# A two-layer trunk kernel: the first 1024 hidden features of each MLP computed plainly, and the recursion's activation operands made during the product that follows

## The chip, the cores and the metric

The kernel runs on one core of a Trainium2 chip. The core has a matrix engine (TensorE, rows PE for matmuls and PEld for weight loads), three elementwise engines (VectorE as DVE, ScalarE as ACT, GpSimd as POOL), and a queue engine (SyncE as SP) from which this kernel issues nearly all its DMAs. Each engine works through its own instructions in order; semaphores tie the engines together. The metric is the device time of one execution in microseconds (us): the median of several runs. A separate, profiled execution gives the trace.

## The reference

A token matrix of 640 tokens (128 context, 512 latent) and 1024 channels passes two layers: a gating mixer in layer 0, an RWKV-7 mixer in layer 1, and after each mixer an MLP with 4096 hidden features. Only the MLP matters here:

```
h = _rmsnorm(x, P['norm2_g'][l]) * (1 + sc2) + sh2
x = x + g2 * (jnp.square(jax.nn.relu(h @ P['mlp_w1'][l])) @ P['mlp_w2'][l])
```

`mlp_w1` is 1024 x 4096, `mlp_w2` 4096 x 1024. Everything is float32.

## The kernel before

**Precision.** Each float32 operand is split into a high part (a cast on ACT into a narrower matmul type) and a low part (a subtraction on DVE). A product is then three matmuls: high x high, high x low, low x high. `mm` issues these three; `split_w` splits weights, `put` splits activations.

**Blocks.** `mlp` walks over the 4096 hidden features in four blocks of 1024. For each block it makes the hidden features (the first product, with `w1`), squares them after a ReLU into `ss`, and multiplies by the block's part of `w2` (the second product, tiles `second_mm`, results added to the residual by `second_out`, L284). A tile is 128 features. A plain tile costs 8 chunks of 128 channels x 3 matmuls x 2 token halves (256 and 384 tokens, `HS`) = 48 matmuls.

**The recursion.** Most of the first product is done by one step of a fast 2x2 matrix recursion: two tiles (a `Pair` of 256 features) come from 7 instead of 8 half-size products, in `pair`, each 4 chunks x 3 matmuls of 320 tokens, together 84 matmuls of 320 columns in place of 96 of 320 columns on average. It needs sums and differences of weight quarters (made on POOL, L475 to L478, and split on ACT and DVE, L452 and L453) and of activation quarters. The activation quarters are made once per layer, in `combos`: for each of four chunk pairs j an add of high and low parts on POOL (m = 0) and on DVE (m = 1), both L596, four DVE adds or subtractions of 320 columns (L600), and a split of 1280 columns back into the tile `Th[j]` (L562 on ACT, L563 on DVE).

**Block 0 before.** Four tiles are plain: in layer 0 tiles 0 to 2 together and then tile 3, in layer 1 tiles 0 and 1 together (`n0`, the number of weight tiles that the previous stage has split already) and then 2 and 3. Then `combos` is called (after the first `n0` tiles in the program), tile 3's results are squared by `first_out` (L626, L627, L562, L563), and features 512 to 1023 come from two pairs, q = 2 and 3. Blocks 1 to 3 use four pairs each. Normalized activations enter in two halves, by `enter`; channel chunks 0 to 3 stand in tiles of their own (`upper`, names ahi and alo), chunks 4 to 7 in slots 1 and 2 of `Th` (name th).

**What sets the order.** Weight tiles go through 5 raw buffers (names wraw), a ring of 3 split buffers (`ring`; names shi and slo, in layer 1 also w1s), and `need(k, i, more)` splits weights ahead by `more` steps. PSUM has three banks `fmps`. The tile framework orders each engine's instructions by priority and readiness in its own model, so the order on an engine is not the order of the source. The scratch `SC` (name bs) holds the normalized activations in `enter` and then the sums of `combos` (half of it for even j, half for odd j).

Of the kernel before, what the change touches and what calls it, by code (L numbers as in the profile page):

```python
# [7 lines left out]
F32 = mybir.dt.float32  # L8
# [7 lines left out]
P = 128  # L16
T = 640
TP = 128
HS = ((0, 256), (256, 640))
KT = 8  # L20
# [8 lines left out]
def tile_trunk(ctx: ExitStack, tc: tile.TileContext, a: dict):  # L29
    nc = tc.nc  # L30
    vec = nc.vector
    act = nc.scalar
# [62 lines left out]
    def parts(pool, tags=("ah", "al")):  # L95
        return pool.tile([P, T], F32R, tag=tags[0], name="ahi"), pool.tile([P, T], F32R, tag=tags[1], name="alo")
# [327 lines left out]
    def mlp(norm, l, ring=None, pre=()):  # L424

        cut = ((0, N2), (N2, T)) if l == 0 else ((N2, T), (0, N2))

        B11, B12, B21, B22 = (0, 1, 2, 3) if l == 0 else (1, 0, 3, 2)
        o0, o1 = (0, 1) if l == 0 else (1, 0)

        SLOT = {1: 0, 2: 1 + l, 3: 2 - l, 5: 3 + B12, 6: 3 + B11, 7: 3 + B22, 4: 3 + B21}
        with ExitStack() as es:
            raw = Pool(es, f"mr{l}", {"r": RAW})
            sp = Pool(es, f"mlps{l}", {"ah": 8, "al": 8})
# [7 lines left out]
            tp = Pool(es, f"mq{l}", {"s": 2})  # L442
            Th = [Pool(es, f"mh{l}{j}", {"t": 1}).tile([P, 2, 7, N2], F32R, "t", "th") for j in range(4)]
# [74 lines left out]

            n0 = len(pre) or 3
            units = []  # L520
            for n in range(4):
                units.append(("p", 0, n, Tile(a["w1"][l, n] if n >= len(pre) else None)))
            units += [("q", 0, q, Pair(0, q)) for q in (2, 3)]
            for b in range(4):
                if b:
                    units += [("q", b, q, Pair(b, q)) for q in range(4)]
# [20 lines left out]
            def need(k, i, more):  # L547
                p = where[k, i] + more
                while count["made"] < len(todo) and count["made"] <= p:
                    ahead()  # L550
                    u, i1, k1, before = todo[count["made"]]
                    for d in before:
                        count["free"] += d.make(0)[1]
                        ahead()
                    made[k1, i1], f = u.make(i1)
                    count["free"] += f
                    count["made"] += 1
                ahead()
# [5 lines left out]

            at = lambda j, i: (Th[j][:, 0, i], Th[j][:, 1, i])

            upper = [parts(sp) for _ in range(4)]
            SC = scr.tile([P, 8, N2], F32, "s", "bs")
            flat = SC.rearrange("p s t -> p (s t)")

            def row(k, t0, t1):
                if k < 4:
                    return [x[:, t0:t1] for x in upper[k]]
                return [Th[k - 4][:, z, 1:3].rearrange("p s t -> p (s t)")[:, t0:t1] for z in range(2)]

            def enter(h):
                r0, r1 = HS[h]
# [7 lines left out]

            def combos():
                for j in range(4):
                    h, w = (y[:, cut[0][0]:cut[0][1]] for y in upper[j])
                    act.copy(Th[j][:, 0, 0], h)
                    vec.tensor_copy(Th[j][:, 1, 0], w)  # L590
                for j in range(4):
                    E = SC[:, 4 * (j % 2):4 * (j % 2) + 4]
                    x = E.rearrange("p s t -> p (s t)")
                    for m in range(2):
                        h, w = row(j + 4 * m, 0, T)
                        (vec if m else nc.gpsimd).tensor_tensor(out=x[:, T * m:T * m + T], in0=h, in1=w, op=ALU.add)  # L596

                    for o, i0, i1, op in ((B22, B22, B12, ALU.subtract), (B12, B12, B11, ALU.subtract),
                                          (B11, B22, B11, ALU.add), (B21, B21, B11, ALU.subtract)):
                        vec.tensor_tensor(out=E[:, o], in0=E[:, i0], in1=E[:, i1], op=op)  # L600
                    put((Th[j][:, 0, 3:7], Th[j][:, 1, 3:7]), E)
# [20 lines left out]
                mm(ps[:, PS0 + t0:PS0 + t1], chunk(w, k), row(k, t0, t1), k == 0, k == 7)  # L622

            def first_out(n, ps, r):
                c = tmps[n % 2][:, 0:r[1] - r[0]]
                act.activation(out=c, in_=ps[:, PS0 + r[0]:PS0 + r[1]], func=AF.Relu)  # L626
                vec.tensor_tensor(out=c, in0=c, in1=c, op=ALU.mult)  # L627
                if n not in ss:
                    ss[n] = parts(sp)
                put([y[:, r[0]:r[1]] for y in ss[n]], c)  # L630
# [46 lines left out]
            need(0, 0, 2)  # L677
            enter(o0)
            fs = [bank() for _ in range(n0)]
            tmps = [tp.tile([P, 512], F32, "s", "ct") for _ in range(2)]  # L680
            ws = [made.pop((m, m)) for m in range(n0)]
            for k in range(KT):
                for m in range(n0):
# [5 lines left out]
            for m in range(n0):  # L689
                first_out(m, fs[m], HS[o0])  # L690
# [3 lines left out]
            for m in range(n0):  # L694
                for k in range(4, KT):
                    first_mm(fs[m], ws[m], k, o1)
                first_out(m, fs[m], HS[o1])
                need(m, m, 3)
            combos()
            for m in range(n0, 4):  # L700
                need(m, m, 1 if m == 3 else 2)
                w, ps = made.pop((m, m)), bank()
                for h in (o0, o1):
                    for k in range(KT):
                        first_mm(ps, w, k, h)
                for h in (o0, o1):
                    first_out(m, ps, HS[h])


            k = 4  # L710
            while k < len(units):
                kind, b, n, u = units[k]
                if kind == "q":
# [5 lines left out]
                if b < 3 or n < 5:  # L719
                    need(k, n, 2)  # L720
                    w, ps = made.pop((k, n)), bank()
# [1198 lines left out]
    with ExitStack() as es:  # L1920
# [15 lines left out]
        for h in (1, 0):  # L1936
            t0, t1 = HS[h]
# [90 lines left out]
```

## Time and profile before

| what | value |
|---|---|
| median of 3 runs (lowest, highest) | 2103.75 us (2103.6, 2108.88) |
| profiled execution, whole | 2122.6 us |
| its span, first to last instruction | 2120.8 us |
| mean granted TensorE clock | 0.927 |
| busy: PE, DVE, ACT, POOL | 92%, 65%, 40%, 27% of the span |
| chain that ended last: PE, DVE, issue, POOL, ACT | 73%, 13%, 5%, 4%, 4% |

The profiled execution took 18.85 us (0.9%) longer than the median of the timed runs. A row of the stage view gives a stretch in us, its length, then for each engine busy time and count, then the granted TensorE clock (1.00 is full), the DMA share and GB/s. A row of the timeline gives start, length, engine, line, operation, what is written from what, and in brackets the idle time before it with what ended it. A row of a group gives busy time and mean ns, a row of a line's view the smallest, median and largest ns. Matmuls overlap, so the pace of TensorE is read from starts and not from lengths. The first MLP stands at 236 to 720 us, the second from 1644 us to the end.

### The profile page before, as it was taken

How to read it: one execution, taken by the hardware profiler on the slowest of the kernel's cores; microseconds unless marked ns; L12 is line 12 of the kernel's file. 1: busy time of each engine (PE TensorE's matmuls, PEld its weight loads, DVE VectorE, ACT ScalarE, POOL GpSimd, SP SyncE). 2: the span in 40 equal slices, each digit the busy share in tenths (PEclk: the TensorE clock that was granted, in tenths of full speed). 3: DMA queues.
4: the chain of work that ended last, by engine and by line, in shares of the span. 5: the costliest groups of instructions: out<-in, count | busy, mean ns of one | idle time of the engine just before them, and what ended most of it. 6: DMA issues, size and time to landing. Idle time of an engine off the chain costs nothing.

```text
span 2120.8 us, 39445 instructions
## 1 busy us (share of the span) xinstructions
PE 1955.6 (92%) x15546; PEld 1696.3 (80%) x15546; DVE 1372.7 (65%) x2706; ACT 853.2 (40%) x1983; POOL 570.6 (27%) x809
## 2 busy tenths in 40 slices
PE   6999969999999879888869999999999799999997
PEld 4777869999999759777657766767787689999997
DVE  5435594646556696765786577787657865656574
ACT  5313542423233255544424445554434633323241
POOL 0000030302030110477642374465301222221210
PEclk9999989999999889987878879998799899999999
DMA  8776103142413124554565445552241122213121
GB/s 282 266 262 223 59 30 100 60 149 70 145 55 129 61 78 137 149 153 145 161 182 155 141 130 167 161 163 77 67 130 60 50 90 69 91 61 99 52 88 50
DMA packets 124442, 254.59 MB, mean 120 GB/s; under 512 B 24417, under 2 KB 63969, under 8 KB 124129
## 3 DMA queue, kind: packets, MB, share of 16 engines
q1 hardware_dynamic: 123824, 251.62, 37.0%
q8 instruction: 122, 2.00, 0.4%
q14 instruction: 64, 0.52, 0.1%
q10 hardware_dynamic: 432, 0.46, 0.1%
HBM read 214.67 MB, written 45.22 MB: 123 GB/s over the span
## 4 chain that ended last, share of the span: by engine, by line
PE 73%; DVE 13%; issue 5%; POOL 4%; ACT 4%; DMA 1%; SPq 0%; POOLq 0%; DVEq 0%; ACTq 0%
PE fmps L114 27%; PE fmps L615 9%; PE zps L311 5%; PE p L1202 4%; PE wops L1472 3%; PE vps L1043 2%; PE za L1331 2%; PE za L1318 2%; PE sy L1345 2%; DVE slo L453 2%; DVE cs L607 1%; PE sy L1326 1%; PE rps L114 1%; PE trps L1224 1%; PE adaps L1458 1%
## 5 line engine op out<-in xcount | busy, mean ns | idle before, releaser
L615 PE MATMUL fmps<-th,shi 128*128 128x320 f32 (+2 forms) x1144 | 258.6, 314 | 28.6 <-ACT ct L626 17.8
L284 DVE SCALAR_TENSOR_TENSOR x<-fmps,mod,x 128x128 f32<-128x128 f32 (+2 forms) x153 | 74.6, 527 | 289.4 <-PE fmps L114 289.4
L615 PEld LDWEIGHTS fmps<-th,shi 128*128 128x128 f32 x1144 | 193.5, 190 | 36.7 <-ACT ct L626 18.1
L452 ACT CAST shi<-wraw 128x1024 fp32r<-128x1024 f32 (+1 forms) x139 | 112.0, 824 | 234.6 <-PE fmps L114 158.8
L615 PE MATMUL fmps<-th,slo 128*128 128x320 f32 (+2 forms) x572 | 178.3, 312 | 0.2 <-DVE slo L453 0.2
L453 DVE TENSOR_TENSOR slo<-wraw,shi 128x1024 fp32r<-128x1024 f32 (+1 forms) x139 | 143.1, 1032 | 30.2 <-ACT shi L452 29.4
L114 PE MATMUL fmps<-ahi,shi 128*128 128x256 f32 (+1 forms) x640 | 151.7, 310 | 0.0
L114 PE MATMUL fmps<-ahi,slo 128*128 128x256 f32 (+1 forms) x640 | 150.9, 309 | 0.0
L114 PE MATMUL fmps<-alo,shi 128*128 128x256 f32 (+1 forms) x640 | 150.9, 309 | 0.0
L114 PE MATMUL fmps<-ahi,w1s 128*128 128x256 f32 (+1 forms) x768 | 148.3, 309 | 0.0
L475 POOL TENSOR_TENSOR s<-wraw 128x512 f32<-128x512 f32 x28 | 38.0, 1360 | 408.4 <-DMA wraw<-w 376.0
L615 PE MATMUL fmps<-th,w1s 128*128 128x320 f32 (+2 forms) x828 | 129.1, 313 | 12.9 <-ACT ct L626 8.9
L615 PEld LDWEIGHTS fmps<-th,w1s 128*128 128x128 f32 x828 | 123.9, 190 | 15.2 <-ACT ct L626 9.2
L1133 POOL TENSOR_TENSOR inv<-inv 128x220 f32<-128x220 f32 (+29 forms) x217 | 100.1, 461 | 114.4 <-DVE inv L1126 57.7
L114 PEld LDWEIGHTS fmps<-ahi,w1s 128*128 128x128 f32 x768 | 127.2, 188 | 0.1
L114 PEld LDWEIGHTS fmps<-ahi,shi 128*128 128x128 f32 x640 | 116.5, 188 | 4.2 <-issue 2.5
L1202 PE MATMUL p<-W,IT 128*128 128x256 f32 x320 | 109.5, 453 | 10.0 <-DVE B L1217 6.0
L114 PEld LDWEIGHTS fmps<-alo,shi 128*128 128x128 f32 x640 | 116.9, 188 | 0.0
L114 PEld LDWEIGHTS fmps<-ahi,slo 128*128 128x128 f32 x640 | 116.9, 188 | 0.0
L1135 POOL TENSOR_TENSOR inv<-inv 128x220 f32<-128x220 f32 (+29 forms) x217 | 106.3, 490 | 16.9
L452 ACT CAST w1s<-wraw 128x512 fp32r<-128x512 f32 (+1 forms) x71 | 57.3, 815 | 132.0 <-PE fmps L114 105.6
L615 PEld LDWEIGHTS fmps<-th,slo 128*128 128x128 f32 x572 | 108.9, 190 | 0.6 <-DVE slo L453 0.6
(345 smaller groups left out, 5042.4 us busy)
## 6 DMA issues: line engine op xcount, KB each, us to landing
wraw<-w SPq DMA_DIRECT2D x126, 512.0 KB, 3.6
wraw<-ada SPq DMA_DIRECT2D x64, 512.0 KB, 4.5
W<-dKR SPq DMA_DIRECT2D x80, 256.0 KB, 3.5
adaw<-adac SPq DMA_DIRECT2D x32, 512.0 KB, 4.4
dKR<-zero SPq DMA_DIRECT2D x32, 320.0 KB, 6.1
dKR<-KR SPq DMA_DIRECT2D x32, 320.0 KB, 4.1
dIT<-IT SPq DMA_DIRECT2D x16, 640.0 KB, 3.4
IT<-dIT SPq DMA_DIRECT2D x80, 128.0 KB, 2.7
```

Of the source, the lines that this page charges most:

```text
L114: pe.matmul(ps[:, PS0 + t0:PS0 + t1], w, x[:, t0:t1], start=start, stop=stop)
L284: vec.scalar_tensor_tensor(out=X[n][:, t0:t1], in0=ps[:, t0 - r[0]:t1 - r[0]], scalar=mod[l][:, which, n, g:g + 1], in1=X[n][:, t0:t1], op ...
L311: pe.matmul(pss[i], x[:, i * P:(i + 1) * P], w[:, kq * 512:(kq + 1) * 512], start=(k == 0 and j == 0), stop=(k == KT - 1 and j == 2))
L452: act.copy(dst[0], x)
L453: vec.tensor_tensor(out=dst[1], in0=x, in1=dst[0], op=ALU.subtract)
L615: pe.matmul(ps, u, v, start=first and z == 0, stop=last and z == 2, **kw)
L1043: pe.matmul(pss[i // 2][:, i % 2], x[:, i * P:(i + 1) * P], w[:, kq * 256:(kq + 1) * 256], start=(k == 0 and j == 0 and i % 2 == 0), stop= ...
L1133: eng.tensor_tensor(out=tv, in0=LA[:, s + 1:32, s:s + 1].to_broadcast([P, n, m]), in1=LX[:, s:s + 1, c0:c1].to_broadcast([P, n, m]), op=AL ...
L1135: eng.tensor_tensor(out=LX[:, s + 1:32, c0:c1], in0=LX[:, s + 1:32, c0:c1], in1=tv, op=ALU.subtract)
L1202: pe.matmul(ps[:, :, 2 * e:2 * e + 2].rearrange("p h s t -> p h (s t)"), IT[:, e], W[:, :, 2 * e:2 * e + 2].rearrange("p h s t -> p h (s t ...
L1318: pe.matmul(za[a0:a0 + 64, 0], W[:, h, 3 * e], RZ[:, ti, h, c], start=True, stop=True)
L1472: pe.matmul(ps, u, v, start=start and j == 0, stop=stop and j == 2)
```

## The change

All eight tiles of block 0 become plain: the two pairs go, four plain tiles with full-width evictions (640 tokens at once, through the scratch `SC`) come. The activation chunks 0 to 3 stand in slots 3 and 4 of `Th` instead of `upper`. `combos` is called after the eighth tile's eviction.

```
             n0 = len(pre) or 3
             units = []
-            for n in range(4):
+            for n in range(KT):
                 units.append(("p", 0, n, Tile(a["w1"][l, n] if n >= len(pre) else None)))
-            units += [("q", 0, q, Pair(0, q)) for q in (2, 3)]
...
-            upper = [parts(sp) for _ in range(4)]
             SC = scr.tile([P, 8, N2], F32, "s", "bs")
             flat = SC.rearrange("p s t -> p (s t)")
 
             def row(k, t0, t1):
-                if k < 4:
-                    return [x[:, t0:t1] for x in upper[k]]
-                return [Th[k - 4][:, z, 1:3].rearrange("p s t -> p (s t)")[:, t0:t1] for z in range(2)]
+                i = 1 if k > 3 else 3
+                return [Th[k % 4][:, z, i:i + 2].rearrange("p s t -> p (s t)")[:, t0:t1] for z in range(2)]
...
                 for j in range(4):
-                    h, w = (y[:, cut[0][0]:cut[0][1]] for y in upper[j])
-                    act.copy(Th[j][:, 0, 0], h)
-                    vec.tensor_copy(Th[j][:, 1, 0], w)
+                    act.copy(Th[j][:, 0, 0], Th[j][:, 0, 3 + B11])
+                    vec.tensor_copy(Th[j][:, 1, 0], Th[j][:, 1, 3 + B11])
...
             def first_out(n, ps, r):
-                c = tmps[n % 2][:, 0:r[1] - r[0]]
+                w = r[1] - r[0]
+                c = (tp.tile([P, 512], F32, "s", "ct") if w < T else flat[:, 1280 * (n % 2):1280 * (n % 2) + T])[:, 0:w]
...
-            combos()
-            for m in range(n0, 4):
-                need(m, m, 1 if m == 3 else 2)
+            for m in range(n0, KT):
+                need(m, m, 2)
                 w, ps = made.pop((m, m)), bank()
                 for h in (o0, o1):
                     for k in range(KT):
                         first_mm(ps, w, k, h)
-                for h in (o0, o1):
-                    first_out(m, ps, HS[h])
-
-
-            k = 4
+                first_out(m, ps, (0, T))
+            combos()
+
+
+            k = KT
```

Line numbers after the change are lower by 3 to 5: L592 and L596 are then what L596 and L600 were, L561 and L562 what L562 and L563 were, L611 what L615 was, L623 and L624 what L626 and L627 were. Outside the two MLPs each engine's instructions stand in the same order before and after. Three places inside them matter.

**First place: VectorE in layer 0, when tiles 0 to 2 are finishing.** slo is a weight's low part, ct the square of a tile, bs the scratch of `combos`, th the operands it leaves. Before:

```order
L596 TENSOR_TENSOR bs_2204<-th_2181 128x640
L600 TENSOR_TENSOR bs_2204<-bs_2204 128x320 x2
L453 TENSOR_TENSOR slo_2467<-wraw_2211,shi_2466 128x1024
L627 TENSOR_TENSOR ct_2276<-ct_2276 128x384
L600 TENSOR_TENSOR bs_2204<-bs_2204 128x320
L453 TENSOR_TENSOR slo_2489<-wraw_2213,shi_2488 128x1024
L563 TENSOR_TENSOR alo_2399<-ct_2276,ahi_2398 128x384
L627 TENSOR_TENSOR ct_2277<-ct_2277 128x384
L600 TENSOR_TENSOR bs_2204<-bs_2204 128x320
```

With the change:

```order
L592 TENSOR_TENSOR bs_2196<-th_2181 128x640
L453 TENSOR_TENSOR slo_2461<-wraw_2203,shi_2460 128x1024
L624 TENSOR_TENSOR ct_2455<-ct_2455 128x384
L453 TENSOR_TENSOR slo_2484<-wraw_2205,shi_2483 128x1024
L562 TENSOR_TENSOR alo_2390<-ct_2455,ahi_2389 128x384
L624 TENSOR_TENSOR ct_2478<-ct_2478 128x384
L453 TENSOR_TENSOR slo_2507<-wraw_2211,shi_2506 128x1024
L562 TENSOR_TENSOR alo_2397<-ct_2478,ahi_2396 128x384
```

The 320-column steps of `combos` are gone from between the weight splits and evictions; the weights of tiles 3, 4 and 5 are split in their place.

**Second place: VectorE in layer 0, where it finishes the first product and passes to the second.** Before, the last steps of `combos` stand among the weight halves of the first pair and ahead of tile 3's eviction (ct_2277):

```order
L563 TENSOR_TENSOR th_2181<-bs_2204,th_2181 128x1280
L600 TENSOR_TENSOR bs_2204<-bs_2204 128x320
L596 TENSOR_TENSOR bs_2204<-th_2189 128x640
L600 TENSOR_TENSOR bs_2204<-bs_2204 128x320 x4
L627 TENSOR_TENSOR ct_2277<-ct_2277 128x256
L600 TENSOR_TENSOR bs_2204<-bs_2204 128x320
L453 TENSOR_TENSOR slo_2623<-wraw_2219,shi_2622 128x512
L563 TENSOR_TENSOR th_2185<-bs_2204,th_2185 128x1280
```

With the change, from the end of tile 6's eviction (alo_2747) on; the square and alo_2808 are tile 7, x0_67 is the residual of the second product's first tile, slo_2852 and slo_2909 are weights of its third and fourth:

```order
L562 TENSOR_TENSOR alo_2747<-bs_2196,ahi_2746 128x640
L596 TENSOR_TENSOR bs_2196<-bs_2196 128x320 x4
L453 TENSOR_TENSOR slo_2852<-wraw_2510,shi_2851 128x1024
L624 TENSOR_TENSOR bs_2196<-bs_2196 128x640
L562 TENSOR_TENSOR th_2177<-bs_2196,th_2177 128x1280
L562 TENSOR_TENSOR alo_2808<-bs_2196,ahi_2807 128x640
L592 TENSOR_TENSOR bs_2196<-th_2185 128x640
L596 TENSOR_TENSOR bs_2196<-bs_2196 128x320 x8
L284 SCALAR_TENSOR_TENSOR x0_67<-fmps_2857,mod0_87,x0_67 128x128
L284 SCALAR_TENSOR_TENSOR x0_67<-fmps_2857,mod0_87,x0_67 128x512
L562 TENSOR_TENSOR th_2181<-bs_2196,th_2181 128x1280
L562 TENSOR_TENSOR th_2185<-bs_2196,th_2185 128x1280
```

`combos` now stands behind tile 6's eviction, around tile 7's, and beside the second product's residuals.

**Third place: VectorE in layer 1, when the first token half has entered.** st and dg belong to the second half's norm, slo to the weights of tile 2. Before:

```order
L226 SCALAR_TENSOR_TENSOR st_17171<-st_17171 128x2
L590 COPY th_17085<-alo_17099 128x320
L563 TENSOR_TENSOR th_17081<-bs_17100,th_17081 128x384
L563 TENSOR_TENSOR th_17085<-bs_17100,th_17085 128x384
L194 TENSOR_TENSOR dg_17170<-cst_85,st_17171 128x256
L453 TENSOR_TENSOR slo_17066<-wraw_17101,shi_17065 128x1024
```

With the change:

```order
L562 TENSOR_TENSOR th_17036<-bs_17047,th_17036 128x384
L562 TENSOR_TENSOR th_17040<-bs_17047,th_17040 128x384
L453 TENSOR_TENSOR slo_17021<-wraw_17048,shi_17020 128x1024
L223 RECIPROCAL st_17116<-st_17116 128x2
L224 TENSOR_TENSOR st_17116<-st_17116 128x2
L225 SCALAR_TENSOR_TENSOR st_17116<-st_17116 128x2
L226 SCALAR_TENSOR_TENSOR st_17116<-st_17116 128x2
L194 TENSOR_TENSOR dg_17115<-cst_85,st_17116 128x256
```

The norm's last step (dg) has moved behind the weight split.

More of the change, by code (lines that the diff above doesn't have):

```diff
@@ L679, in mlp @@
             fs = [bank() for _ in range(n0)]
-            tmps = [tp.tile([P, 512], F32, "s", "ct") for _ in range(2)]
             ws = [made.pop((m, m)) for m in range(n0)]
```

## Prediction

> **What bounds the kernel now.** I read the chain that ended last first. In this stretch its longest pieces are TensorE, except in one place per layer, just ahead of the second product of block 0. So I cut both places into stages: tile 3 (plain), the two pairs, then the second product; layer 0 first.
>
> ```profile
> 274.74:281.77 7.03, 7.03 (x49) 7.03 (x49) 7.00 (x13) 4.24 (x7) 2.17 (x2) 1.00 0.22 75
> 281.77:327.21 45.44, 27.51 (x171) 26.98 (x171) 38.48 (x50) 18.86 (x34) 14.32 (x9) 0.77 0.18 58
> 327.21:383.53 56.32, 56.32 (x387) 56.32 (x386) 19.86 (x30) 9.53 (x12) 7.76 (x6) 1.00 0.21 66
> 1675.04:1681.82 6.78, 6.78 (x46) 6.78 (x47) 6.70 (x9) 3.26 (x6) 5.02 (x1) 1.00 0.22 79
> 1681.82:1725.56 43.74, 29.55 (x172) 27.96 (x171) 32.69 (x49) 19.68 (x37) 14.85 (x10) 0.84 0.19 60
> 1725.56:1781.88 56.32, 56.32 (x386) 56.32 (x386) 21.26 (x31) 10.30 (x13) 7.77 (x6) 1.00 0.23 73
> ```
>
> The first number after the stretch is its length, the next TensorE's busy time. Plain tiles and the second product are full at clock 1.00; a plain tile takes 7.03 us, a tile of the second product 56.32 / 8 = 7.04. The two pairs take 45.44 and 43.74 us, busy only 27.51 and 29.55, at clocks 0.77 and 0.84. The second product leaves VectorE idle: 19.86 of 56.32 us busy. The gaps in the pairs:
>
> ```profile
> 303.26 0.90 PE L615 MATMUL fmps<-th,shi 128*128 128x320 f32 x2 [17.82 <-ACT ct L626]
> 1692.64 0.64 PE L615 MATMUL fmps<-th,w1s 128*128 128x320 f32 x1 [8.89 <-ACT ct L626]
> 1704.08 0.82 PE L615 MATMUL fmps<-th,shi 128*128 128x320 f32 x2 [4.96 <-ACT cs L649]
> 319.91 7.30 PE fmps L615 x48
> ```
>
> TensorE waits 17.82 us for a PSUM bank whose ReLU stands on ScalarE behind the big casts of `combos`, which wait for VectorE. The last row, of the chain, gives the undisturbed pace of a pair: 7.30 / 48 = 0.152 us a matmul, so 168 matmuls would be 25.6 us. The layers lose 19.9 and 18.2 us there. What VectorE did in layer 0 meanwhile:
>
> ```profile
> L600 DVE TENSOR_TENSOR bs<-bs 128x320 f32<-128x320 f32 x16 | 9.7, 624 | 0.0
> L563 DVE TENSOR_TENSOR th<-bs,th 128x1280 fp32r<-128x1280 f32 x4 | 7.0, 1758 | 0.4 <-ACT th L562 0.4
> L596 DVE TENSOR_TENSOR bs<-th 128x640 f32<-128x640 f32 x4 | 6.9, 1756 | 0.0
> ```
>
> That is 23.6 us of `combos` between 268 and 305 us, the bound of the place.
>
> **The change, part by part.** *Removed and added on TensorE.* Two pairs go (45.44 and 43.74 us as they ran), four plain tiles come: 4 x 7.03 = 28.12 us, if fed. Without any stall in either version the plain tiles would cost 28.1 against 25.6, so the arithmetic alone loses 2.5 us a layer. With the stalls: **-17.3 us in layer 0, -15.6 in layer 1**.
>
> *Are tiles 4 to 7 fed?* Each needs one weight split and one eviction per 7.03 us. A full-width eviction is four passes; from the rows below, 640 columns cost about 0.7 us per ScalarE pass and 0.83 per VectorE pass (the 640-column add's median). ScalarE 1.05 + 2 x 0.7, VectorE 1.2 + 2 x 0.83: under 3 us of 7 on each. The split of tile m + 3 waits only until tile m leaves the ring, two tiles ahead of its use. The raw loads ahead of tile 7 are the same eight as before, in the same order on SP (four tiles and two pairs are eight loads too), and the later ones follow the splits, one per tile. I cost all this at nothing, hidden under the tiles; if one split came a microsecond late, that tile would cost that microsecond.
>
> *Is combos hidden?* Only if nothing that TensorE needs stands behind it. The first product's tile 7 does: its low half is channel chunk 7 of the second product, wanted 7/8 x 7.04 = 6.2 us after that product starts (call that start E).
>
> ```profile
> L596 POOL TENSOR_TENSOR bs<-ahi,alo x8: 1542/2065/6372, 265.6 to 1683.1; 128x640 f32<-128x640 f32 x8
> L596 DVE TENSOR_TENSOR bs<-th x8: 812/826/2187, 269.4 to 1680.9; 128x640 f32<-128x640 f32 x8
> L600 DVE TENSOR_TENSOR bs<-bs x32: 476/480/1815, 272.3 to 1687.4; 128x320 f32<-128x320 f32 x32
> L453 DVE TENSOR_TENSOR slo<-wraw,shi 128x1024 fp32r<-128x1024 f32 x2 | 2.4, 1210 | 0.0
> 292.77 1.48 DVE L563 TENSOR_TENSOR th<-bs,th 128x1280 fp32r<-128x1280 f32 x1
> 296.64 1.68 DVE L600 TENSOR_TENSOR bs<-bs 128x320 f32<-128x320 f32 x4
> L452 ACT CAST shi<-wraw 128x1024 fp32r<-128x1024 f32 x6 | 6.3, 1052 | 4.6 <-PE fmps L615 4.3 <-ACT cs L660 0.3
> L562 ACT CAST th<-bs 128x1280 fp32r<-128x1280 f32 x4 | 5.0, 1262 | 10.5 <-DVE bs L600 10.5
> L626 ACT ACTIVATE ct<-fmps 128x384 f32<-128x384 f32 x4 | 1.9, 487 | 1.2 <-DVE alo L563 1.2
> ```
>
> By the new order: tile 6 ends at E - 7.0; split 1.05 and ReLU 0.7 on ScalarE, square 0.83, cast 0.7 and low half 0.83 bring its eviction to about E - 2.9. POOL's add for j = 0 (2.07) ends at E - 0.8, the four L600 (1.68) at E + 0.9. Tile 7: ScalarE splits 1.05 (waiting for TensorE until E), ReLU until E + 1.8; VectorE's weight half until 2.3, square until 3.1, big subtraction (1.48) until 4.6, low half until 5.4. About 0.8 us spare, eaten by a dozen handovers. But POOL's next add is released when the big subtraction ends, and so runs beside the low half. The L600 row shows 476 ns at least and 1815 at most, and each slow one lies beside a POOL instruction: 1.3 us more. Bounds 0 to 1.5 us a layer; I take **+0.6 us a layer**. [...]
>
> *Behind tile 7* VectorE has the rest of `combos` (about 12 us beside POOL's three adds, each with a full wait) and three residuals. The weights of the second product's third tile stand ahead of it; those of the fourth are due at E + 21, and end by the same adding at about E + 17. The bank of its first tile is wanted only by its fourth. So nothing there; what is late next is these fourth weights, 4 us away.
>
> *The entry in layer 1.* The norm's last step is now behind a weight split, and TensorE's broadcast of it two chunks later:
>
> ```profile
> 1654.33 1.23 DVE L453 TENSOR_TENSOR slo<-wraw,shi 128x1024 fp32r<-128x1024 f32 x1
> 1655.62 0.38 PE L203 MATMUL ssps<-dg,ones 128*128 128x256 f32 x1
> 1665.73 0.39 PE L615 MATMUL fmps<-th,shi 128*128 128x256 f32 x1 [0.33 <-DVE th L563]
> 1666.92 0.39 PE L615 MATMUL fmps<-th,shi 128*128 128x256 f32 x1 [0.58 <-DVE th L563]
> 1675.04 0.44 PE L615 MATMUL fmps<-ahi,w1s 128*128 128x384 f32 x1 [1.14 <-DVE w1s L453]
> ```
>
> The second half enters about 2 us later, and the two waits of 0.33 and 0.58 grow by about 1 us together; VectorE's first low half comes third in its queue, not first, some 0.5 us. Against that the 1.14 us ahead of tile 3 go, since no L600 stands ahead of that split. I take **0, between -1.5 and +1.5**. Layer 0's entry keeps its order.
>
> **The sum:** -17.3 - 15.6 + 0.6 + 0.6 + 0 = -31.7 us on the profiled execution of 2122.6 (span 2120.8, 1.8 around it): 2090.9. The median of the timed runs is 0.991 of that execution, so -31.4: **2072 us**.
>
> **The rivals.**
> *A late tail.* If tile 7's low half is late by more than a short stall, the clock falls too. What a gap costs:
>
> ```profile
> 245.87 0.38 PE L615 MATMUL fmps<-ahi,shi 128*128 128x256 f32 x1 [1.41 <-ACT ahi L562]
> 245.87:250.00 4.13, 4.03 (x17) 3.63 (x18) 2.86 (x8) 4.13 (x12) 0.00 (x0) 0.60 0.01 4
> ```
>
> A gap of 1.41 us, with thin work behind it, gave 4.13 us at 0.60: 1.7 us lost beyond the gap; the gap of 1.14 us at 1675.04 was followed by clock 1.00. [...] A stall of 1.5 us with it is 3.2 a layer. If POOL's add for j = 0 takes its largest, 6.37, everything behind moves by 4.3 us: a stall of 3.5 to 4.1 and about 2 of clock, 6 a layer. Against: VectorE waits for that add, so it runs undisturbed (1.54 at least). So 5 to 11 us more in all: **2077 to 2083**.
>
> *Starved weights.* If all of `combos` beside POOL takes the 23.6 us that it took before, the fourth tile's weights come some 5 us late and the next ones also: with the tail, 10 us a layer: **about 2091**.
>
> *The wait only moves: slower.* Place: the four L600 on VectorE ahead of tile 7's square. If they wait for POOL as long as the pairs waited before, the stall of 19.9 and 18.2 us returns at chunk 7 of the second product, and the plain arithmetic's 2.5 us a layer is added: +5 us, **2109**. It decides if tile 7's low half comes later than E + 6.2 + 17 in layer 0. For it: the queue is in order and POOL is slow. Against: one add of at most 6.4 us stands there, not four.
>
> *Half done.* If the order left most of `combos` where it was, little would go; the rows show it moved, except the four copies and two 640-column adds.
>
> **How the numbers follow.** Forecast (2068 to 2077) 0.67; late tail 0.15; starved weights 0.05; wait moved 0.03; half or another unseen loss, 2097 to 2110, 0.04; more than forecast, since a fuller TensorE spares a clock fall, 2062 to 2068, 0.06. About 0.3%, 6.3 us, is what a measurement can tell from no change. Faster by that 0.93, within 0.04, slower 0.03. Range **2064 to 2085**: forecast, late tail and the near part above forecast.
>
> **What would show it.** After the change: tiles 3 to 7 at 7.03 us each with clock 1.00; the second product of block 0 starting about 17 us earlier in layer 0 and some 33 earlier in layer 1; a stall, if any, at chunk 7 of that product's first tile, on DVE alo; L596 and L600's successors inside that product. Wrong if TensorE idles over 2 us in it, if a plain tile waits on a split, or if block 1's first pair waits for th.

## The result and the profile after

The changed kernel takes **2075.55 us** (median; 2069.75 to 2083.24) against 2106.32 us for the kernel before on the same chip: ratio **0.9849**, 95% interval 0.98 to 0.9899. The forecast was 2072, range 2064 to 2085. Its profiled execution has a span of 2067.9 us. In its chain that ended last TensorE has 78% (73% before), VectorE 11% (13%).

The stage view of the kernel after, with columns as in the prediction, for tiles 3 to 7 and the second product of block 0, layer 0 first:

```profile
274.06:309.24 35.18, 35.18 (x242) 35.18 (x241) 15.54 (x21) 11.88 (x16) 1.56 (x1) 1.00 0.30 99
309.24:365.56 56.32, 56.32 (x386) 56.32 (x385) 34.41 (x46) 14.57 (x16) 16.43 (x9) 1.00 0.18 57
1637.93:1673.11 35.18, 35.06 (x240) 34.92 (x239) 16.95 (x23) 13.08 (x19) 1.57 (x1) 1.00 0.35 105
1673.11:1729.43 56.32, 56.32 (x386) 56.32 (x385) 36.14 (x47) 15.31 (x17) 16.53 (x9) 1.00 0.20 62
```

Five plain tiles take 35.18 us, 7.04 each, at clock 1.00. The second product is as long as before, 56.32, with VectorE now busy for 34.41 of it (19.86 before): `combos` lies there, and TensorE doesn't notice. Against tile 3 and the two pairs before (7.03 + 45.44, 6.78 + 43.74) that is 17.3 and 15.3 us less.

The closest place is the end of the first product. The timeline of VectorE, GpSimd and TensorE in layer 0, where the second product starts at 309.24 (E):

```profile
307.07 1.56 POOL L592 TENSOR_TENSOR bs<-th 128x640 f32<-128x640 f32 x1 [305.87 <-DVE alo L562]
308.66 2.07 DVE L596 TENSOR_TENSOR bs<-bs 128x320 f32<-128x320 f32 x4 [1.77 <-POOL bs L592]
312.52 1.49 DVE L562 TENSOR_TENSOR th<-bs,th 128x1280 fp32r<-128x1280 f32 x1
313.92 0.82 DVE L562 TENSOR_TENSOR alo<-bs,ahi 128x640 fp32r<-128x640 f32 x1
314.08 4.19 POOL L592 TENSOR_TENSOR bs<-th 128x640 f32<-128x640 f32 x2 [5.46 <-DVE th L562]
314.65 2.19 DVE L592 TENSOR_TENSOR bs<-th 128x640 f32<-128x640 f32 x1
315.69 0.45 PE L114 MATMUL fmps<-alo,shi 128*128 128x256 f32 x2
327.53 1.21 DVE L453 TENSOR_TENSOR slo<-wraw,shi 128x1024 fp32r<-128x1024 f32 x1
333.79 1.49 DVE L562 TENSOR_TENSOR th<-bs,th 128x1280 fp32r<-128x1280 f32 x1 [1.39 <-ACT th L561]
```

Tile 7's low half ends at 314.74, 0.95 us ahead of the first matmul that reads it, at 315.69; the fourth tile's weights end at 328.74, 1.6 us ahead of E + 21.1; the last of `combos` ends at E + 26, 30 us before block 1's first pair (365.56).

Two larger numbers need care. Between the two profiled executions lie 52.9 us of span, more than the medians' 30.8. The stage view of both, for layer 0's MLP (first broadcast of the norm to the last matmul), the mixer of layer 1, and layer 1's MLP (statistics of the second token half to the last broadcast; those of the first half come 11 us earlier and count to the mixer here). Before:

```profile
239.71:718.54 478.83, 452.10 (x3009) 438.40 (x3008) 286.17 (x464) 170.12 (x316) 85.79 (x61) 0.97 0.27 88
718.54:1647.00 928.46, 843.97 (x8046) 656.71 (x8045) 682.60 (x1545) 429.93 (x1225) 389.75 (x680) 0.87 0.43 130
1647.00:2111.26 464.26, 439.87 (x2923) 434.06 (x2923) 284.60 (x463) 169.83 (x309) 94.40 (x60) 0.98 0.22 69
```

After:

```profile
239.59:700.76 461.17, 451.95 (x3033) 438.53 (x3032) 268.38 (x435) 163.63 (x294) 74.85 (x52) 1.00 0.27 91
700.76:1611.16 910.40, 828.67 (x8044) 647.25 (x8045) 684.36 (x1548) 431.22 (x1227) 387.88 (x680) 0.88 0.43 133
1611.16:2058.66 447.50, 438.41 (x2946) 433.36 (x2946) 272.13 (x435) 164.15 (x289) 80.60 (x52) 1.00 0.22 72
```

The MLPs give 17.7 and 16.8 us; another 18.1 come from the mixer, which the change doesn't touch. And at the mixer's start something is given back. The timeline of its first matmul on TensorE and of the step that VectorE takes ahead of it, before:

```profile
724.63 0.77 PE L799 MATMUL l1ps<-xq,wraw 128*128 128x255 f32 x1 [6.09 <-issue]
716.84 2.31 DVE L211 TENSOR_TENSOR h<-x,ssps 128x256 f32<-128x256 f32 x5 [1.06 <-PE fmps L114]
```

After:

```profile
708.39 1.19 PE L794 MATMUL l1ps<-xq,wraw 128*128 128x255 f32 x2 [7.63 <-issue]
700.62 1.75 DVE L211 TENSOR_TENSOR h<-x,ssps 128x256 f32<-128x256 f32 x5 [2.62 <-PE fmps L114]
```

TensorE waits 1.5 us longer, since VectorE's normalization waits 1.56 us longer for a matmul of the MLP. The matmul that ends just before the normalization starts is, before:

```profile
716.47 0.33 PE L114 MATMUL fmps<-alo,shi 128*128 128x384 f32 x1
```

After:

```profile
700.24 0.33 PE L114 MATMUL fmps<-alo,shi 128*128 128x384 f32 x1
```

Both read the low half of a square in the MLP's last tile. The first is the eleventh matmul from the end (chunk 4 of 0 to 7), the second the last but one (chunk 7); three chunks of three matmuls at 0.17 us are the 1.56 us. It is the same in all profiles below: chunk 4 where layer 0 keeps its pairs in block 0, chunk 7 where they are gone.

### The profile page after: what moved, and what is told of

The parts are those of the page before. It is cut to its first block, busy times and chain, and to the rows that moved or that the text cites. A ratio compares the mean times of both kernels' runs of the same rounds, so it can differ in the third digit from the quotient of the medians.

```text
span 2067.9 us, 39399 instructions
## 1 busy us (share of the span) xinstructions
PE 1938.2 (94%) x15594; PEld 1685.9 (82%) x15594; DVE 1344.3 (65%) x2652; ACT 842.3 (41%) x1945; POOL 543.9 (26%) x793
## 4 chain that ended last, share of the span: by engine, by line
PE 78%; DVE 11%; ACT 4%; issue 3%; POOL 3%; DMA 1%; SPq 0%; DVEq 0%; ACTq 0%; POOLq 0%
PE fmps L114 27%; PE fmps L611 13%; PE zps L311 5%; PE p L1197 4%; PE wops L1467 4%; PE vps L1038 3%; PE za L1326 2%; PE za L1313 2%; PE rps L114 2%; PE sy L1340 2%; DVE slo L453 1%; PE sy L1321 1%; PE trps L1219 1%; PE adaps L1453 1%; DVE cs L603 1%
## 5 line engine op out<-in xcount | busy, mean ns | idle before, releaser
L611 PE MATMUL fmps<-th,shi 128*128 128x320 f32 (+2 forms) x1208 | 270.5, 312 | 9.8 <-ACT th L561 4.1
L611 PEld LDWEIGHTS fmps<-th,shi 128*128 128x128 f32 x1208 | 202.8, 189 | 18.8 <-ACT th L561 5.7
L611 PE MATMUL fmps<-th,slo 128*128 128x320 f32 (+2 forms) x604 | 187.2, 310 | 0.0
L114 PE MATMUL fmps<-ahi,shi 128*128 128x256 f32 (+1 forms) x704 | 166.4, 310 | 0.0
L114 PE MATMUL fmps<-ahi,slo 128*128 128x256 f32 (+1 forms) x704 | 165.5, 309 | 0.0
L114 PE MATMUL fmps<-alo,shi 128*128 128x256 f32 (+1 forms) x704 | 165.4, 309 | 0.0
L611 PE MATMUL fmps<-th,w1s 128*128 128x320 f32 (+2 forms) x972 | 150.0, 312 | 4.0 <-DVE cs L658 3.4
L611 PEld LDWEIGHTS fmps<-th,w1s 128*128 128x128 f32 x972 | 144.6, 189 | 6.6 <-DVE cs L658 5.2
L114 PEld LDWEIGHTS fmps<-alo,shi 128*128 128x128 f32 x704 | 128.6, 188 | 0.0
L592 POOL TENSOR_TENSOR bs<-th 128x640 f32<-128x640 f32 x8 | 17.0, 2133 | 421.5 <-DVE alo L562 305.9
L114 PE MATMUL fmps<-ahi,w1s 128*128 128x256 f32 (+1 forms) x640 | 124.1, 309 | 0.0
L475 POOL TENSOR_TENSOR s<-wraw 128x512 f32<-128x512 f32 x24 | 32.5, 1356 | 329.7 <-DMA wraw<-w 283.6
L611 PEld LDWEIGHTS fmps<-th,slo 128*128 128x128 f32 x604 | 114.2, 189 | 0.0
L452 ACT CAST w1s<-wraw 128x1024 fp32r<-128x1024 f32 (+1 forms) x66 | 54.9, 836 | 131.4 <-PE fmps L114 81.8
```

Of the source, the lines that this page charges most:

```text
L114: pe.matmul(ps[:, PS0 + t0:PS0 + t1], w, x[:, t0:t1], start=start, stop=stop)
L452: act.copy(dst[0], x)
L611: pe.matmul(ps, u, v, start=first and z == 0, stop=last and z == 2, **kw)
```

## The experiments

The theory (W): what the change earns is the wait in block 0's pairs, and nothing else moves. Rivals: the mixer gains through the clock; the order on ScalarE, not VectorE's work, made the wait; eight plain tiles alone would have done; the place of `combos` is of no account. Each run was timed against the kernel before on its chip. The stage lengths in us are from each kernel's stage view, the rest from the timed runs:

| run | MLP 0 | mixer | MLP 1 | median us | ratio (95% interval) |
|---|---|---|---|---|---|
| e1 the change again | 459.7 | 915.4 | 448.4 | 2078.25 | 0.9872 (0.9851, 0.9893) |
| e11 and again | 461.0 | 918.0 | 448.9 | 2078.91 | 0.9865 (0.9837, 0.9894) |
| e2 layer 0 alone | 462.3 | 914.3 | 463.5 | 2092.3 | 0.9936 (0.9915, 0.9957) |
| e3 layer 1 alone | 478.1 | 914.9 | 448.5 | 2092.05 | 0.9929 (0.9906, 0.9951) |
| e5 the kernel before again | 477.8 | 906.9 | 463.7 | 2107.57 | 0.9989 (0.9971, 1.0007) |
| e4 pairs, no combos | 462.4 | 908.5 | 452.0 | 2086.67 | 0.9903 (0.9878, 0.9927) |
| e6 combos behind tile 3 | 479.9 | 909.4 | 462.4 | 2109.58 | 1.0005 (0.9986, 1.0023) |
| e7 extra combos early | 470.7 | 909.7 | 456.9 | 2096.17 | 0.993 (0.9907, 0.9954) |
| e8 combos before tile 7 | 468.1 | 916.6 | 454.7 | 2093.04 | 0.9916 (0.989, 0.9942) |
| e10 adds on VectorE | 461.1 | 905.8 | 448.0 | 2076.21 | 0.9844 (0.9811, 0.9876) |
| e9 buffers turned | 462.1 | 918.2 | 448.7 | 2079.76 | 0.9856 (0.9828, 0.9884) |
| e12 ring turned | 459.7 | 918.0 | 448.8 | 2076.21 | 0.9826 (0.9795, 0.9858) |

**e1 and e11, the change again** (no edit).

> The changed kernel once more, timed against the kernel before on one chip. In the two profiled executions the MLPs gave 17.8 us in layer 0 and 16.8 us in layer 1, and the layer-1 mixer between them, which nothing in the change touches, was shorter by another 18.1 us (928.5 to 910.4 us from the end of layer 0's last matmul to layer 1's first stats). Theory W (only the wait for the bank goes; the mixer's 18 us are two executions that differ by themselves): ratio 0.983 to 0.986, 30 to 35 us, and the mixer somewhere between 905 and 930 us. Rival C (a fuller TensorE in layer 0's MLP changes the granted clock in the mixer behind it): about 52 us, ratio 0.975, and the mixer again near 910 us.

> The changed kernel a third time, beside e9 on one chip. The traces say: MLPs 33 us less (17.2 and 15.7), 1.5 us given back at the mixer's start, so 31 us in all, ratio 0.985. Rival D (more than that is given back in the mixer, as the 27.9 us of e1 could mean): ratio above 0.9875, and a mixer that is longer than in the profiles of the kernel before by more than the 1.5 us at its start.

The MLPs repeat: 461.2, 459.7, 461.0 in layer 0 and 447.5, 448.4, 448.9 in layer 1. The mixer doesn't: 910.4, 915.4, 918.0. The medians are 27.9 and 28.9 us below the kernel before, short of the 30 to 35 that e1 expected. Rival C's 52 us are out. Rival D is not: 0.9872 is at its bound, and e11's 0.9865 reaches it only by its interval.

**e2 and e3, one layer alone.** The code of both versions, chosen by layer (e3 has `l == 1`):

```
+            full = l == 0
+            for n in range(KT if full else 4):
...
+            if not full:
+                combos()
+            for m in range(n0, KT if full else 4):
...
+            if full:
+                combos()
```

> The change in layer 0 alone; layer 1 has its two pairs and the early combos as before. Theory W: layer 0's MLP 17.8 us shorter, layer 1's MLP with its gaps of 8.9 and 5.0 us back; together 17 to 18 us less than before, ratio near 0.9915. Rival C: the mixer behind layer 0's MLP is shorter too, by about 18 us: 36 us less, ratio near 0.983.

> The change in layer 1 alone. Theory W: layer 0's gap of 17.8 us back, layer 1's MLP 16.8 us shorter; 16 to 17 us less than before, ratio near 0.992. Rival C says the same of the time, since the mixer stands ahead of this MLP, but the mixer must then take as long as in the kernel before, about 928 us; a mixer near 910 us here speaks against C.

The timeline of TensorE where each keeps its pairs; e2 in layer 1:

```profile
1661.59 0.64 PE L617 MATMUL fmps<-th,w1s 128*128 128x320 f32 x1 [8.87 <-ACT ct L629]
```

And e3 in layer 0:

```profile
302.56 0.90 PE L617 MATMUL fmps<-th,shi 128*128 128x320 f32 x2 [17.77 <-ACT ct L629]
```

The old waits are back to 0.05 us, and only in that layer. The medians are 13.9 and 14.1 us below the kernel before, 28.0 together, as in e1: the two layers add. Both are about 3 us short of what was expected (17 to 18 and 16 to 17). In the stage lengths, against the mean of both profiles of the kernel before (478.3 and 464.0), e2 gains 16.0 us in MLP 0 and e3 15.5 in MLP 1. e3 decides against C: its layer 0 is the old one, yet its mixer takes 914.9 us, far from 928.5.

**e5, the kernel before again** (no edit).

> The kernel before once more, for a second profile. In the profiles so far the MLPs give 33 to 35 us together, but the timed runs of e1 give 22 to 31 us. Theory S (the profile of before was a slow execution of the mixer only; its MLPs repeat): layer 0's MLP again 478 to 479 us and layer 1's 464 us, gaps of 17.8, 8.9 and 5.0 us at the same places, and a mixer of 908 to 918 us. Rival B (the stall itself is shorter in most executions, and the profile of before overstated it): layer 0's MLP under 475 us or layer 1's under 461.

```profile
240.50:718.28 477.78, 450.99 (x3009) 437.08 (x3008) 285.47 (x464) 170.02 (x316) 86.03 (x61) 0.97 0.26 88
718.28:1625.20 906.92, 826.16 (x8044) 645.33 (x8045) 680.27 (x1545) 429.31 (x1225) 389.40 (x680) 0.89 0.43 133
1625.20:2088.89 463.69, 439.34 (x2922) 434.13 (x2922) 284.88 (x463) 169.90 (x309) 94.37 (x60) 0.98 0.21 69
```

The stage view again: the MLPs are within 1.1 us of the first profile of before, the mixer 21.5 us shorter on the same program, at clock 0.89 for 0.87. Theory S holds, with layer 0's MLP and the mixer a little under its figures: the 18 us between the first two profiles say nothing of the change.

**e4, pairs without combos.** From the kernel before:

```
             def combos():
                 for j in range(4):
-                    h, w = (y[:, cut[0][0]:cut[0][1]] for y in upper[j])
...
-                    put((Th[j][:, 0, 3:7], Th[j][:, 1, 3:7]), E)
+                    for c0, c1 in ((0, 1), (3, 7)):
+                        nc.gpsimd.memset(Th[j][:, :, c0:c1].bitcast(F32), 0.0)
```

> The kernel before with its pairs in block 0, but combos left out: GpSimd only clears the slots that it would fill, so the recursion works on zeros there and the output is not the reference's. It measures the two pairs without the wait. Theory W as predicted (the plain arithmetic loses 2.5 us a layer): the two pairs take 25.6 us in each layer, without a gap over 1 us, against 28.1 for four plain tiles; time 38 us less than before, ratio near 0.982, some 3 to 5 us better than the change. Rival P (the pairs wait for their weights even without combos): 28 us or more for the pairs of a layer, with gaps that DVE slo or ACT shi ends, and a time no better than the change's.

The timeline around the first pair of layer 0 on TensorE, VectorE and ScalarE (L614 and L615 here are L626 and L627 of before):

```profile
288.33 0.63 PE L603 MATMUL fmps<-th,shi 128*128 128x320 f32 x1 [3.33 <-ACT ct L614]
282.47 2.95 DVE L453 TENSOR_TENSOR slo<-wraw,shi 128x512 fp32r<-128x512 f32 x2 [1.84 <-ACT shi L452]
285.34 1.48 DVE L615 TENSOR_TENSOR ct<-ct 128x256 f32<-128x256 f32 x1
283.71 0.38 ACT L614 ACTIVATE ct<-fmps 128x256 f32<-128x256 f32 x1
286.85 0.40 ACT L562 CAST ahi<-ct 128x256 fp32r<-128x256 f32 x1 [2.25 <-DVE ct L615]
287.79 0.49 ACT L614 ACTIVATE ct<-fmps 128x384 f32<-128x384 f32 x1 [0.53 <-DVE alo L563]
```

The stage view of e4: the first pair with its wait, the stretch behind it, the rest of both pairs, and both pairs of layer 1:

```profile
281.33:288.33 7.00, 3.67 (x25) 3.40 (x24) 5.17 (x6) 2.98 (x7) 5.05 (x4) 0.93 0.23 74
288.33:293.83 5.50, 5.50 (x20) 5.50 (x21) 3.06 (x6) 2.08 (x5) 0.00 (x0) 0.50 0.28 97
293.83:312.59 18.76, 18.64 (x126) 18.37 (x125) 13.94 (x23) 9.96 (x19) 2.72 (x2) 0.99 0.27 84
1647.71:1678.70 30.99, 24.68 (x154) 24.16 (x152) 24.00 (x34) 14.66 (x29) 8.65 (x6) 0.89 0.27 85
```

The two pairs take 31.26 us in layer 0 (7.00 + 5.50 + 18.76) and 30.99 in layer 1. A pair claims all three banks `fmps`, one of which is tile 3's. That tile is squared in two halves through one scratch: the second ReLU, at 287.79, waits until VectorE has finished with the first half. VectorE is late with it because two weight halves of the pair stand ahead of the square, and because these rows run beside GpSimd's sums for the pair's weights (L475 to L478; GpSimd is busy for 5.05 of the 7.00 us): 1.48 us for a square of 256 columns, against 0.41 in the kernel before at 298.25, where GpSimd rests. So TensorE stops for 3.33 us and then runs 5.50 at clock 0.50; in layer 1 the same gap, at 1655.09, is 6.19 us. Theory W's pairs without a gap are refuted, and the kernel is 19.5 us faster than the one before, not 38. Rival P's length holds (28 us or more). Its cause holds in part: what ends the gap is the bank, which neither expected, but work on the pair's weights delays the bank. Pairs behind a tile 3 that is evicted at full width weren't run. Without any `combos`, this kernel is still about 8 us behind the change on its chip (2086.67 and 2078.25).

**e6, combos behind tile 3's eviction.** From the kernel before:

```
-            combos()
             for m in range(n0, 4):
...
                 for h in (o0, o1):
                     first_out(m, ps, HS[h])
+            combos()
```

> The kernel before with one line moved: combos stands behind tile 3's eviction in the program, so that on ScalarE tile 3's ReLU goes ahead of three of the four big casts; the pairs and all else stay. Theory A (the order on ScalarE is the cause: the bank waits for a ReLU queued behind casts that wait for VectorE): the 17.8 us gap falls below 6 us, but the first pair then meets casts that are not done, so part returns inside it; 15 to 30 us less than before for both layers. Theory V (the 24 us that VectorE and GpSimd need for combos are the bound, wherever the ReLU stands): the two pairs of layer 0 still end near 325 us, within 4 us of before, only with the gap at another instruction; time within 8 us of before.

The timeline of TensorE in the pairs of layer 0 (its waits alone):

```profile
296.88 0.90 PE L615 MATMUL fmps<-th,shi 128*128 128x320 f32 x2 [10.04 <-ACT ct L626]
302.32 0.63 PE L615 MATMUL fmps<-th,shi 128*128 128x320 f32 x1 [3.48 <-ACT th L562]
303.85 0.63 PE L615 MATMUL fmps<-th,shi 128*128 128x320 f32 x1 [0.89 <-DVE th L563]
305.59 0.63 PE L615 MATMUL fmps<-th,shi 128*128 128x320 f32 x1 [0.85 <-ACT th L562]
307.12 0.63 PE L615 MATMUL fmps<-th,shi 128*128 128x320 f32 x1 [0.89 <-DVE th L563]
```

The 17.8 us become 10.04 at the bank and 6.1 at `th` itself; the time is the same (1.0005). In layer 1 the 8.89 and 4.96 us become 3.39 at the bank, 6.83 at a weight half and 3.3 at `th`. Tile 3's first ReLU goes ahead of three of the four big casts, as meant; the second, which frees the bank, goes ahead of two and still waits for VectorE to finish the first half. Theory V: a better order on ScalarE only renames the wait, because the pairs need what VectorE is still making.

**e7, the change with extra combos early.** An `extra()`, a copy of `combos` that writes into two unused slots, at the old place; evictions in halves:

```
-                c = (tp.tile([P, 512], F32, "s", "ct") if w < T else flat[:, 1280 * (n % 2):1280 * (n % 2) + T])[:, 0:w]
+                c = tp.tile([P, 512], F32, "s", "ct")[:, 0:w]
...
+            extra()
             for m in range(n0, KT):
...
-                first_out(m, ps, (0, T))
+                for h in (o0, o1):
+                    first_out(m, ps, HS[h])
             combos()
```

> The change, and beside its late combos the same work once more at the old place (ahead of tile 3 in the program), written into two slots that nothing reads, with evictions in two halves; the result is the reference's. It asks whether eight plain tiles alone would have done. Theory L (what counts is that combos is late): the early copy delays evictions and weight splits of tiles 4 to 7 and TensorE idles 8 us or more a layer between tiles 3 and 7; 16 to 40 us more than the change. Theory K (a plain tile takes one bank, and there are three, so an eviction may be two tiles, 14 us, late, while a pair takes all three at once): at most 4 us a layer; within 10 us of the change.

The stage view of tiles 3 to 7 and of the second product in layer 0:

```profile
274.10:309.44 35.34, 35.34 (x242) 35.34 (x242) 33.87 (x56) 17.96 (x32) 15.70 (x4) 1.00 0.27 90
309.44:375.23 65.79, 59.87 (x386) 59.15 (x386) 35.29 (x48) 15.69 (x20) 12.53 (x8) 0.92 0.17 57
```

The timeline of TensorE at its wait:

```profile
321.29 0.58 PE L114 MATMUL fmps<-ahi,shi 128*128 128x256 f32 x1 [5.53 <-ACT ahi L561]
```

Both theories are half right. With VectorE busy for 33.87 of 35.34 us, layer 0's plain tiles still run without a wait: one bank each out of three lets evictions lag (K); tile 4's last ReLU comes 10 us after its last matmul. But the debt falls due at tile 7's eviction: 5.53 us, and 65.79 instead of 56.32. In layer 1 it falls due sooner: the entry up to tile 3 takes 30.95 us for 26.77 to 28.16 in the change's three profiles, and tiles 3 to 7 take 39.73 for 35.18, with a weight 2.95 us late. This kernel gains 11.6 us on the kernel before on its chip, the change 27.9 to 30.8 on its own: 16 to 19 us are lost, which is more than K allowed. So the late place counts (L), though TensorE idles less between tiles 3 and 7 than L said. The halved evictions are part of this run and weren't measured apart.

**e8, combos ahead of tile 7's eviction:**

```
+                if m == KT - 1:
+                    combos()
                 first_out(m, ps, (0, T))
-            combos()
```

> The change with combos one step earlier in the program, ahead of tile 7's eviction and not behind it: the rival in which the wait only moves, made real. Tile 7's square then stands behind the last sums of combos on VectorE, and its low half is wanted 6.2 us after the second product starts. Theory W: in the change the last of combos ended 26 us after that start with other work between; here tile 7's low half comes 18 to 22 us after it, so TensorE stops for 12 to 16 us at chunk 7 of the first tile of the second product, with a clock fall of about 2 us behind it; 28 to 36 us for both layers, a time within 8 us of the kernel before. Rival (VectorE has room enough, the place of combos within this product is of no account): under 3 us of gap, time as the change's.

The stage view of the second product in both layers, and of the stretch behind layer 0's wait:

```profile
311.78:374.18 62.40, 57.90 (x385) 57.64 (x385) 31.34 (x43) 13.46 (x15) 12.42 (x8) 0.97 0.15 51
1688.66:1751.33 62.67, 59.25 (x387) 58.99 (x386) 35.13 (x44) 14.46 (x16) 11.25 (x8) 0.95 0.17 56
328.59:333.00 4.41, 4.41 (x21) 4.41 (x22) 2.15 (x4) 0.86 (x1) 0.00 (x0) 0.67 0.00 0
```

The timeline of TensorE and VectorE at that wait:

```profile
328.59 0.90 PE L114 MATMUL fmps<-ahi,shi 128*128 128x256 f32 x2 [4.50 <-ACT ahi L561]
329.36 0.82 DVE L562 TENSOR_TENSOR alo<-bs,ahi 128x640 fp32r<-128x640 f32 x1
```

Tile 7's low half ends 18.4 us after the second product's start, as expected, 12 us after it was wanted. But the product is only 6.1 and 6.4 us longer, and the kernel still gains 14.7 us on the one before. The reason is in the order on TensorE, around what was the first tile's chunk 7 (fmps_2857 is the first tile, fmps_2914 the second; ahi_2746 is chunk 6, ahi_2847 chunk 7):

```
L114 MATMUL fmps_2857<-ahi_2746,slo_2690 128x384
L114 MATMUL fmps_2914<-ahi_2389,shi_2750 128x256
...
L114 MATMUL fmps_2914<-ahi_2746,slo_2751 128x256
L114 MATMUL fmps_2857<-ahi_2847,shi_2689 128x256
```

Seven chunks of the second tile stand ahead of the first tile's chunk 7. The trace agrees: TensorE works for 12.3 us, 14 chunks of 0.88, before it stops at 324.09. That the scheduler saw chunk 7 late in its own model is the likely reason for the order; no run shows it. Neither expectation had that.

**e10, the adds on VectorE:**

```
-                        (vec if m else nc.gpsimd).tensor_tensor(out=x[:, T * m
+                        vec.tensor_tensor(out=x[:, T * m
```

> The change with the adds of high and low parts for chunk m = 0 on VectorE and not on GpSimd, so that GpSimd does nothing in combos. It asks what the two cost each other, and what the room behind tile 7 is worth. Theory W: the slow VectorE rows beside GpSimd (2.19 us for an add of 640 columns, up to 1.8 for one of 320) go back to 0.82 and 0.48; the first add stands ahead of tile 7's square but takes 0.82 us, so its low half still comes some 0.7 us or more before it is wanted, no gap; combos ends within 4 us of where it ended; time within 3 us of the change. Rival (VectorE has no room for four more adds): gaps over 1 us in block 0's second product, 3 us or more a layer.

The groups of VectorE's adds in `combos` (busy us, mean ns, then idle time before them), and the spread of the 640-column adds (smallest, median, largest ns), in the change:

```profile
L592 DVE TENSOR_TENSOR bs<-th 128x640 f32<-128x640 f32 x8 | 12.0, 1506 | 0.1
L596 DVE TENSOR_TENSOR bs<-bs 128x320 f32<-128x320 f32 x32 | 14.4, 486 | 6.6 <-POOL bs L592 6.4
L592 DVE TENSOR_TENSOR bs<-th x8: 820/1506/2194, 267.2 to 1689.3; 128x640 f32<-128x640 f32 x8
```

In e10:

```profile
L592 DVE TENSOR_TENSOR bs<-th 128x640 f32<-128x640 f32 x16 | 12.5, 820 | 0.1
L596 DVE TENSOR_TENSOR bs<-bs 128x320 f32<-128x320 f32 x32 | 14.4, 485 | 0.3
```

Without GpSimd beside it VectorE does 16 adds in 12.5 us; with it, 8 in 12.0 (four at 0.82 while GpSimd rests, four at 2.19 beside it), and 6.4 us of waiting. So GpSimd's half of the adds saved VectorE 0.5 us and cost it 6.4. The MLPs take as long as with the change, and the time is e11's on the same chip within 3 us (2076.21 and 2078.91): all of it is hidden there.

**e9 and e12, the 1.5 us at the mixer's start.** The change with four pairs of square tiles taken and left unused, or one weight tile of layer 0's ring:

```
+            for _ in range(4):
+                parts(sp)
             ss = {}
...
+            if l == 0:
+                ring()
             need(0, 0, 2)
```

> The change with one addition: four pairs of square tiles are taken from their pool and left unused, so that the eight squares of block 0 lie in the same buffers as in the kernel before (there the first four of the pool had held the upper activation chunks). It asks for the cause of 1.5 us that every kernel with the change in layer 0 gives back: TensorE waits 7.6 us ahead of the mixer's first matmul, against 6.1 in the others. Theory M (the mixer's first normalized tiles lie over a square that is read last): the wait is 6.1 us again, and the mixer's first matmul comes 1.5 us sooner after layer 0's last; the rest as the change, a time 1 to 2 us less, which a few rounds cannot tell. Rival (something else in the order at the end of layer 0): the wait stays at 7.6 us.

> The change, with one weight tile of layer 0's ring taken and left unused, so that the last weight tile of that MLP lies in the ring buffer that it had in the kernel before (there block 0 took 12 tiles from the ring of 3, with the change 8). Second theory for the 1.5 us that come back at the mixer's start, after e9 left the wait at 7.65 us. Theory N (the mixer's first normalized tile lies over the weights that the last matmul reads): VectorE's first h starts before TensorE's last matmul of layer 0 ends, and the wait ahead of the mixer's first matmul is 6.1 us again. Rival: it stays at 7.6 us and the cause stays open. The time is 0 to 2 us less than the change's, which a few rounds cannot tell.

The timeline of the mixer's first matmul in e9:

```profile
710.20 1.19 PE L796 MATMUL l1ps<-xq,wraw 128*128 128x255 f32 x2 [7.65 <-issue]
```

In e12:

```profile
708.22 1.19 PE L796 MATMUL l1ps<-xq,wraw 128*128 128x255 f32 x2 [7.64 <-issue]
```

The wait stays in both, and the matmul that lets VectorE go is chunk 7's in both. So neither theory is borne out, as far as the unused tiles turn the buffers as meant, which no trace shows. The wait is 7.6 in e2 too, where only layer 0 is changed, and 6.1 in e3, so it hangs on layer 0's change. Why the normalization waits for a square's low half at all, and for another chunk after the change, stays open.

## Why the prediction was right

The direction, the cause and the size hold. By its steps:

- **The bound.** VectorE's work for `combos` held the pairs: e6 moves the ReLU and gains nothing, and e4 leaves `combos` out and keeps 3.33 of layer 0's 17.82 us.
- **Removed and added on TensorE:** forecast -17.3 and -15.6, measured -17.3 and -15.3. This is nearly the whole result.
- **"The arithmetic alone loses 2.5 us a layer"** was wrong as a picture of the alternative. It held for pairs "without any stall", and e4 shows that they have one without `combos` too: 31.3 and 31.0 us against 28.1, so plain tiles gain 3. The step put the whole gap down to the casts of `combos`; without them 3.33 of the 17.82 us remain in layer 0 and 6.19 of 8.89 + 4.96 in layer 1, from handing tile 3's bank to a pair. The sum didn't use it; the rival "the wait only moves" did, for its +5.
- **Tile 7's low half:** forecast E + 5.4, measured E + 5.5. The stall of 0.6 us a layer was mis-sized: it is 0. GpSimd's next add was released at 314.08, beside the low half, but that took its usual 0.82 us; the add behind it took 2.19.
- **The fourth weights:** forecast E + 17, measured E + 19.5. The 4 us of room were 1.6.
- **The entry in layer 1:** forecast 0, between -1.5 and +1.5. From the second half's statistics to tile 3's start it is 28.04 us before (1647.00 to 1675.04) and 26.77 after (1611.16 to 1637.93), but 26.76 in e5 and 27.61 and 28.16 in e1 and e11: on average 0.1 us more with the change. The granted clock of that stretch was 0.89 in the 28.04 us before and 0.94 in the 26.77 after. The terms were partly wrong: the 1.14 us ahead of tile 3 go, but the waits of 0.33 and 0.58 shrink, to 0.19 and 0.31, where they were to grow by 1 us.
- **Not in the sum:** the 1.5 us given back behind layer 0's MLP.
- **The signs.** The second product starts 18.0 us earlier in layer 0 (327.21 and 309.24), as forecast. In layer 1 it starts 52.5 us earlier (1725.56 and 1673.11) and not 33: 18.1 of that are the mixer's.
- **The sum.** With the mean of two profiles of before (478.3, 464.0) and three of the change (460.6, 448.3), the MLPs give 17.7 + 15.7 = 33.4 us, less 1.5: 31.9, against the forecast's 31.7. That it comes so close is partly luck: the 1.2 us of stall that didn't come nearly cancel the 1.5 that nobody had forecast. The medians give 30.8, 27.9 and 28.9, and 28.1 and 33.5 in e9 and e12, which only leave a buffer unused: 29.8 on average, 2 us less than the profiles. Those 2 us would be in the mixer, whose length spreads from 905.8 to 928.5 over the 14 profiles whatever was changed; whether part of the gain is given back there is not settled.
- **The rivals.** "The wait only moves" was wrong also in its price. e8 made it: tile 7 came 12 us late and cost 6.1 to 6.4 us a layer, because other matmuls had been put ahead of its chunk on TensorE. That is the size the late tail was given (6 us a layer), by another path.

## What to carry to other kernels

Work that one engine makes for a later stage belongs in a stage where that engine idles, even at the price of more matmuls: here 192 that were fed took 28.1 us a layer, 168 that waited 45.4 and 43.7, and the second product stayed at 56.32 us in layer 0 with VectorE busy for 34.41 of it and not 19.86. Before costing the faster form at its pace, ask what it claims at its start: here a pair takes all three banks `fmps` at once, while plain tiles ran on with an eviction 10 us late (e7). And when two profiles differ, compare the untouched stages first: 18 of the 53 us here were one of them.

## What the runs showed of the hardware

- Clock falls followed gaps of very different lengths: 3.33 us of waiting in e4 was followed by 5.50 us at 0.50, 4.50 us in e8 by 4.41 us at 0.67, and before the change 1.41 us by 4.13 us at 0.60, of which TensorE was busy for 4.03. The 1.14 us ahead of tile 3 in layer 1 before the change were followed by 6.78 us at 1.00.
- The same program's mixer took 928.5 us in one profile and 906.9 in another, at mean clocks 0.87 and 0.89, while its MLPs agreed within 1.1 us.
- Sharing out adds to GpSimd was worth next to nothing here: 17.0 us of GpSimd's time in the change relieved VectorE of 0.5 us (e10). An add of 640 columns on VectorE took 0.82 us alone and up to 2.19 beside GpSimd.
